# Down projection of a hybrid decoder layer: one group of nine block pairs in place of four, with its operands made ahead of time

## The chip, the cores and the metric

The kernel runs on one core of a Trainium2 chip. The metric is the device time of one launch in microseconds (us). Three runs of the kernel before took 1814.7, 1817.64 and 1820.21 us, so its median is 1817.64 us.

## The reference

One decoder layer over 1024 tokens and 16 learned tokens ahead of them, all in float32. The part that the change touches is the last line but one: the feed-forward network, whose inner width is 2816 (22 blocks of 128).

```python
h = h + concat([stick_breaking_attention, ssd_mixer, mla_attention]) @ w_out
fn = rmsnorm(h, ffn_norm_g)
h = h + (silu(fn @ w_gate) * (fn @ w_up)) @ w_down     # w_down: 2816 x 1024
return rmsnorm(h, final_norm_g)
```

## The kernel before

**Stages.** The kernel runs through these stages in order, with some overlap: projections and the stick-breaking attention, called the attention stage here (scores from 85 to 463 us), whose gaps on TensorE are filled with the projections of the convolution (`conv_unit`, 12 units); the state-space part (501 to 659 us); the second attention (MLA, 690 to 1024 us); the output projection; gate and up projection, called the gate stage (matmuls of `GateUp` from 1108.6 to 1555 us); the down projection, called the down stage (1555 to 1755 us); and the last part, which does four remaining blocks of the down projection and the final norm (to 1817 us). Tokens lie along the free dimension, features on the 128 partitions.

**Products.** A float32 operand is split into `hi` (ScalarE, called ACT, casts it to the type that TensorE multiplies) and `lo` (the rest, a subtraction on VectorE, called DVE, or on GpSimd, called POOL). A product is three matmuls: hi·hi, lo·hi and hi·lo.

**Gate and down stage.** Both use a scheme that multiplies 2 x 2 blocks with seven products instead of eight, at the price of sums of the blocks. The products carry the numbers 1 to 7. For the down projection a block pair `p` is two blocks of 128 of the inner width: the weights `w_down[2p]`, `w_down[2p+1]` (each 128 x 1024, two halves) and the hidden rows of the same two blocks. Product 1 takes plain blocks; 2 and 3 take plain inputs, 2 and 4 plain weights; the others take sums of blocks. One product of a pair is 12 matmuls of 128 x 512 into four PSUM banks (`product`).

**The gate stage's units.** `GateUp(p)`, p = 0 to 10, makes the hidden rows of pair p. `out(q)` ends each quarter: a sigmoid on ACT, two multiplications on DVE, and a store of the quarter `gs` to `s_hid` in DRAM from the queue of SyncE, called SP. The quarters end in the order 0, 3, 1, 2.

**The down stage.** `down_group(p0, n)` runs four times, with 2, 2, 2 and 3 pairs. It loads raw weights and hidden rows of its pairs (512 KB each), makes the sums for one product after another on DVE (`sub` and `add`, L1081 and L1084, in place in `raw` and in the tiles `tt`), splits both operands (casts on ACT L1077; `lo` of the weights on POOL L1078, of the inputs on POOL or DVE, by `LO_DVE`), and after each product adds the four banks into the residual `hF` on DVE (`gather`, L1084, with the loop `for o in range(4)`). Product 1 goes to `E1`, which POOL adds to `hF` at the end of all groups. Matmuls: L1496 to L1498.

**Order.** Every engine and the SP queue do their instructions in the order of the program. That order is set by a scheduler that places instructions by a priority (mostly the order in the code) and by its own estimate of when each is ready. A tile's tag with `bufs` buffers is handed out in turn: a new user waits until the last one is done. The value loads of the attention (`load_value_steps`) stage their raw data in two tiles, tags `vst` and `vsp`, one buffer each.

Of the kernel before, what the change touches and what calls it, by code (L numbers as in the profile page):

```python
# [21 lines left out]
KT = D // 128  # L22
# [36 lines left out]
def tile_hybrid_block(ctx: ExitStack, tc: tile.TileContext, a: dict):  # L59
# [588 lines left out]
    with ctx_sb as st:  # L648
# [27 lines left out]
        def sb_attend(p, proj, values):  # L676
            Q, K, KS = proj
            for h in range(2):
                for j in range(NQ // 2):
                    rows = [sb_row(Q[h], K[h], KS[h], 2 * j + e) for e in range(2)]  # L680
                    weighted_values(tp, pvp, sbb, j, rows, values[0], h, [x[p, 64 * h : 64 * (h + 1)] for x in (s_osbh, s_osbl)], pms[j % 2], values[1])

        values = load_value_steps(sbv, sbb, 0)
        step_sizes()
        convs = [8, 9, 10, 11, 0, 1, 2, 3, 4, 5, 6, 7]
        for p in range(4):
            sb_attend(p, proj, values)
# [548 lines left out]
    class GateUp:  # L1236


        def __init__(self, p):
            self.p = p  # L1240
            self.before = {}
            self.w, self.raw = [], []

        def load_early(self):
# [191 lines left out]
    f2 = ctx.enter_context(tc.tile_pool(name="f2", bufs=1, reuse_waits="tile"))  # L1436
    nraw = nop = 0

    def next_raw(src):
        nonlocal nraw  # L1440
        pl = fr if nraw % 16 < 8 else f2
        nraw += 1
        return raw_tile(pl, src)

    def operand():
        nonlocal nop
        t = fo.tile([128, 1024], F32R, tag="op", bufs=4, name="op") if nop % 16 >= 12 else hid_tile("op")
        nop += 1
        return t[:, HALF[0]], t[:, HALF[1]]
# [5 lines left out]
    LO_DVE = (1, 6, 2)  # L1455

    def down_group(p0, n):
        W, H = [], []
        for e in range(n):
            w, h = ([next_raw(src[2 * (p0 + e) + i]) for i in range(2)] for src in (a["w_down"], s_hid))  # L1460
            W.append((w[0][:, HALF[0]], w[1][:, HALF[0]], w[0][:, HALF[1]], w[1][:, HALF[1]], q_tile("tt")))
            H.append((h[0][:, HALF[0]], h[0][:, HALF[1]], h[1][:, HALF[0]], h[1][:, HALF[1]], q_tile("tt")))

        def operands(i):
            out = []
            for (a11, a12, a21, a22, tw), (b11, b12, b21, b22, th) in zip(W, H):
                if i == 6:
                    sub(a21, a11, a21)
                    sub(b12, b22, b12)
                    sub(tw, a22, a21)  # L1470
                    add(th, b12, b11)
                elif i == 5:
                    add(a11, tw, a11)
                    sub(b11, b22, th)
                elif i == 3:
                    sub(a12, a12, tw)
                elif i == 4:
                    sub(th, b21, th)
                left = {1: a11, 6: tw, 2: a12, 5: a11, 7: a21, 3: a12, 4: a22}[i]
                right = {1: b11, 6: th, 2: b21, 5: b11, 7: b12, 3: b22, 4: th}[i]  # L1480
                if p0 == 0 and i == 1:
                    hl = [wa.tile([128, 1024], F32R, tag=f"w{x}", name=f"w{x}") for x in ("hi", "lo")]
                    pair = [[t[:, s] for t in hl] for s in HALF]
                else:
                    pair = [operand(), operand()]
                split(*pair[0], left, pool)
                split(*pair[1], right, dve if i in LO_DVE else pool)
                out.append(pair)
            return out

        def product(i, banks, start):
            for e, ((wh, wl), (hh, hl)) in enumerate(operands(i)):
                for o in range(4):
                    os = slice(128 * o, 128 * (o + 1))
                    first, last = start and e == 0, e == n - 1
                    pe.matmul(banks[o], wh[:, os], hh, start=first, stop=False, skip_group_check=not start)  # L1496
                    pe.matmul(banks[o], wl[:, os], hh, start=False, stop=False, skip_group_check=not start)  # L1497
                    pe.matmul(banks[o], wh[:, os], hl, start=False, stop=last, skip_group_check=not start)  # L1498

        lo, hi = HALF  # L1500
        A = banks4()
        product(1, A, True)
        if p0 == 0:
            for k in range(KT):
                sp.dma_start(hT[k], s_h[k])
        for o in range(4):
            if p0 == 0:
                act.copy(E1[o], A[o])
            else:
                add(E1[o], E1[o], A[o])  # L1510
        B = banks4()
        product(6, B, True)
        gather(B, 4, lo)
        product(2, A, False)
        gather(A, 0, lo)
        product(5, B, False)
        gather(B, 4, hi)
        C = banks4()
        product(7, C, True)
        gather(C, 4, hi)  # L1520
        product(3, B, False)
        gather(B, 0, hi)
        product(4, C, False)
        gather(C, 4, lo)

    p0 = 0
# [10 lines left out]
    for e, f in enumerate(range(2 * p0, NF)):  # L1537
        w, h = next_raw(a["w_down"][f]), next_raw(s_hid[f])
        if e < 2:
            hl = [wa.tile([128, 1024], F32R, tag=f"w{x}", name=f"w{x}") for x in ("hi", "lo")]  # L1540
            split(*hl, w, pool)
            W = [[t[:, s] for t in hl] for s in HALF]
        else:
            W = [operand() for _ in HALF]
            for x, s in zip(W, HALF):
                split(*x, w[:, s], pool)
        H = [operand() for _ in HALF]
        for x, s in zip(H, HALF):
            split(*x, h[:, s], dve)
        last.append((W, H))  # L1550

    def down(o, t0, n):
        ts = slice(t0, t0 + n)
# [166 lines left out]
```

## Time and profile before

| what | number |
|---|---|
| runs | 1814.7, 1817.64, 1820.21 us |
| profiled execution | 1819.26 us, of which the trace's span is 1817.3 us |
| busy over the span | PE 95%, PEld 83%, DVE 67%, ACT 47%, POOL 47% |
| mean granted TensorE clock | 0.972 |
| bytes moved | 186.93 MB, mean 103 GB/s |
| chain that ended last | PE 68%, DVE 17%, ACT 4%, issue 3%, DMA 3%, POOL 3% |

PE is TensorE's matmuls, PEld its weight loads, which run beside the matmuls. A busy PE isn't a PE at its peak, since matmuls overlap: where nothing waits, the matmuls of 128 x 512 follow each other at less time than each one's own length. So the number of matmuls in a stretch, not its busy share, tells how far PE was held up there.

### The profile page before, as it was taken

What the parts mean: (1) busy time and instruction counts of PE and PEld (TensorE: products, weight loads), DVE (VectorE), ACT (ScalarE), POOL (GpSimd) and SP (SyncE); (2) the same over time, 40 slices, a digit from 0 to 9 for tenths busy, and PEclk for the clock granted to TensorE, in tenths of its full rate; (3) what the DMA queues carried; (4) which work ended last, traced back from release to release, by engine and by line L of the source; (5) the groups of instructions that cost most, each with busy time, mean ns of one, the idle gap of its engine ahead of it and who ended that gap; (6) DMA issues with size and microseconds to landing.
All of it is one profiled execution on the core that took longest, in us unless ns stands there. A gap on an engine that the chain in (4) does not pass through costs nothing.

```text
span 1817.3 us, 26447 instructions
## 1 busy us (share of the span) xinstructions
PE 1722.8 (95%) x9769; PEld 1506.0 (83%) x9769; DVE 1214.3 (67%) x1801; ACT 860.0 (47%) x1878; POOL 858.4 (47%) x597
## 2 busy tenths in 40 slices
PE   7969999999999999999999998999999999799997
PEld 7859998999987778998888876778888888677787
DVE  8686655777544673455576558967776667899854
ACT  7545564555566646775544424422232223334333
POOL 4433334343366557563321345634333234678783
PEclk9969999999998999999999998999999999899999
DMA  4211232222443546347221342232222233733102
GB/s 157 60 53 44 78 88 73 64 70 66 116 148 106 187 159 171 103 124 263 78 88 53 108 140 102 64 99 83 80 76 81 71 98 140 286 100 95 47 1 93
DMA packets 121012, 186.93 MB, mean 103 GB/s; under 512 B 21986, under 2 KB 81412, under 8 KB 120884
## 3 DMA queue, kind: packets, MB, share of 16 engines
q1 hardware_dynamic: 101488, 169.69, 29.6%
q10 hardware_dynamic: 19396, 15.56, 2.8%
q8 instruction: 77, 1.26, 0.3%
q14 instruction: 51, 0.42, 0.1%
HBM read 131.61 MB, written 53.60 MB: 102 GB/s over the span
## 4 chain that ended last, share of the span: by engine, by line
PE 68%; DVE 17%; ACT 4%; issue 3%; DMA 3%; POOL 3%; SPq 1%; ACTq 0%; DVEq 0%; POOLq 0%
PE d_ps L142 8%; PE d_ps L143 8%; PE d_ps L144 8%; PE b_ps L1295 7%; PE b_ps L1297 7%; PE b_ps L1296 7%; DVE raw L1081 2%; PE ptg L317 2%; PE b_ps L1498 1%; PE b_ps L1497 1%; PE ptg L319 1%; PE pv L295 1%; PE b_ps L1496 1%; PE pv L296 1%; DVE hF L1084 1%
## 5 line engine op out<-in xcount | busy, mean ns | idle before, releaser
L142 PE MATMUL d_ps<-hnh,whi 128*128 128x384 f32 (+6 forms) x744 | 247.3, 333 | 1.4 <-DVE go L534 0.7
L144 PE MATMUL d_ps<-hnl,whi 128*128 128x384 f32 (+6 forms) x744 | 246.7, 332 | 0.0
L143 PE MATMUL d_ps<-hnh,wlo 128*128 128x384 f32 (+6 forms) x744 | 245.6, 330 | 0.0
L131 POOL TENSOR_TENSOR wlo<-wraw,whi 128x1024 fp32r<-128x1024 f32 (+1 forms) x57 | 135.9, 2385 | 212.0 <-ACT whi L129 203.1
L1078 POOL TENSOR_TENSOR op<-raw,op 128x512 fp32r<-128x512 f32 x83 | 125.2, 1534 | 42.1 <-ACT op L1077 38.9
L142 PEld LDWEIGHTS d_ps<-hnh,whi 128*128 128x128 f32 (+1 forms) x744 | 140.4, 189 | 5.5 <-DVE go L534 1.3
L144 PEld LDWEIGHTS d_ps<-hnl,whi 128*128 128x128 f32 (+1 forms) x744 | 140.6, 189 | 3.3 <-issue 1.0
L143 PEld LDWEIGHTS d_ps<-hnh,wlo 128*128 128x128 f32 (+1 forms) x744 | 140.4, 189 | 2.3 <-issue 0.2
L1295 PE MATMUL b_ps<-T,wh 128*128 128x512 f32 x352 | 138.4, 393 | 0.9 <-DVE u L1084 0.9
L1296 PE MATMUL b_ps<-T,wl 128*128 128x512 f32 x352 | 138.1, 392 | 0.0
L1297 PE MATMUL b_ps<-T,wh 128*128 128x512 f32 x352 | 138.0, 392 | 0.0
L303 DVE TENSOR_TENSOR pl<-ptg,ph 128x512 fp32r<-128x512 f32 (+1 forms) x160 | 99.6, 628 | 46.3 <-ACT ph L302 44.7
L1078 POOL TENSOR_TENSOR wlo<-raw,whi 128x1024 fp32r<-128x1024 f32 (+1 forms) x22 | 52.7, 2395 | 152.9 <-ACT whi L1077 152.9
L669 DVE TENSOR_TENSOR_SCAN cm<-cm,zcol 128x144 f32<-128x144 f32 (+3 forms) x64 | 103.9, 1634 | 17.8 <-ACT cm L667 17.4
L1077 ACT CAST op<-raw 128x512 fp32r<-128x512 f32 x107 | 61.4, 618 | 96.7 <-PE d_ps L1498 49.4
L302 ACT CAST ph<-ptg 128x512 fp32r<-128x512 f32 (+1 forms) x160 | 85.3, 541 | 36.3 <-PE ptg L319 24.7
L1078 POOL TENSOR_TENSOR wl<-raw,wh 128x512 fp32r<-128x512 f32 x46 | 69.8, 1526 | 58.8 <-ACT wh L1077 58.0
L1084 DVE TENSOR_TENSOR hF<-hF,b_ps 128x512 f32<-128x512 f32 (+1 forms) x96 | 59.2, 635 | 46.4 <-PE b_ps L1562 23.9
L486 DVE SCALAR_TENSOR_TENSOR cacc<-d_ps,cw,cacc 128x384 f32<-128x384 f32 (+3 forms) x108 | 61.8, 572 | 38.2 <-ACT cacc L479 36.2
L1077 ACT CAST wh<-raw 128x512 fp32r<-128x512 f32 x88 | 52.9, 616 | 67.0 <-PE b_ps L1297 64.0
L129 ACT CAST whi<-wraw 128x1024 fp32r<-128x1024 f32 (+1 forms) x57 | 58.9, 1033 | 49.4 <-PE d_ps L144 23.4
L1496 PE MATMUL b_ps<-op 128*128 128x512 f32 x183 | 72.8, 401 | 9.9 <-DVE hF L1084 6.2
(452 smaller groups left out, 5352.8 us busy)
## 6 DMA issues: line engine op xcount, KB each, us to landing
raw<-in_w_gate_dram SPq DMA_DIRECT2D x22, 512.0 KB
raw<-in_w_up_dram SPq DMA_DIRECT2D x22, 512.0 KB, 4.1
s_hid<-gs SPq DMA_DIRECT2D x44, 256.0 KB, 2.4
raw<-in_w_down_dram SPq DMA_DIRECT2D x22, 512.0 KB, 5.2
raw<-s_hid SPq DMA_DIRECT2D x22, 512.0 KB, 4.3
wraw<-in_w_o_dram SPq DMA_DIRECT2D x16, 512.0 KB, 4.0
wraw<-in_w_xbc_dram SPq DMA_DIRECT2D x12, 512.0 KB, 3.8
s_xs<-csig SPq DMA_DIRECT2D x24, 192.0 KB, 2.6
```

What stands on the lines that cost most here:

```text
L131: pool.tensor_tensor(lo[:, :cols], raw[:, :cols], f32(hi[:, :cols]), op=ALU.subtract)
L142: pe.matmul(ps[:m, :n], wh, mh, start=(kt == 0), stop=False)
L143: pe.matmul(ps[:m, :n], wl, mh, start=False, stop=False)
L144: pe.matmul(ps[:m, :n], wh, ml, start=False, stop=(kt == nkt - 1))
L303: dve.tensor_tensor(pl[:, :n], pt[:, :n], f32(ph[:, :n]), op=ALU.subtract)
L669: dve.tensor_tensor_scan(rev, rev, zcol.to_broadcast([128, n_all]), 1.0, ALU.mult, ALU.add)
L1077: act.copy(hi, value)
L1078: eng.tensor_tensor(lo, value, f32(hi), op=ALU.subtract)
L1295: pe.matmul(banks[j], hi[:, ks], UH[u][k], start=start and k == 0, stop=False, skip_group_check=skip)
L1296: pe.matmul(banks[j], lo[:, ks], UH[u][k], start=False, stop=False, skip_group_check=skip)
L1297: pe.matmul(banks[j], hi[:, ks], UL[u][k], start=False, stop=stop and k == 3, skip_group_check=skip)
L1496: pe.matmul(banks[o], wh[:, os], hh, start=first, stop=False, skip_group_check=not start)
```

## The change

**In the attention stage** a new function `down_sums(p, c)` is called three times after each `conv_unit`, for 36 units in all (9 pairs, 4 column blocks). Each loads two pieces of `w_down` (128 KB each), makes the four sums of weights with four POOL operations of 128 x 128, and stores them (256 KB) in `s_wsum`. Its tile shares the tags `vst` and `vsp`.

**In the gate stage** `out` of the first nine units keeps its quarters `gs` and calls `hid_sums(q)`: four POOL operations of 128 x 512 make the sums of the inputs in place, and seven stores of 256 KB go to `s_hops` where four went to `s_hid`.

**In the down stage** there is one group of nine pairs. `operands(i, p)` loads one tile of 128 x 1024 for each product of each pair: the weights of that product on the left (from `w_down`, or from `s_wsum` in runs of 512 bytes) and its inputs on the right (from `s_hops`), two DMAs of 256 KB. One ACT cast makes `hi` for both, POOL makes `lo` of the weights, DVE `lo` of the inputs. No sums are left here, and `gather` runs 7 times, not 28. The order of the products is 1, 6, 2, 5, 7, 3, 4 as before, but each runs over all nine pairs. POOL's additions of `E1` to `hF` move from the end to behind product 1.

```diff
-    s_hid = dram.tile([NF, 128, SEQ], F32, name="s_hid")
+    s_hops = dram.tile([NS, 8, 128, 512], F32, name="s_hops")
+    s_wsum = dram.tile([NS, 4, 128, 4, 128], F32, name="s_wsum")
+    s_hid = dram.tile([NF - 2 * NS, 128, SEQ], F32, name="s_hid")
...
+        def down_sums(p, c):
+            w = sbb.tile([128, 5, 2, 64], F32, tag=("vst", "vsp")[c % 2], bufs=1, name="wd")
+            w = w.rearrange("p b h d -> p (b h d)")[:, :512].rearrange("p (q n) -> p q n", q=4)
+            for e in range(2):
+                src = a["w_down"][2 * p + e].rearrange("p (h c n) -> p h c n", h=2, c=4)
+                sp.dma_start(w[:, e::2], src[:, :, c])
+            for out, x, y, op in ((2, 0, 2, ALU.subtract), (3, 3, 2, ALU.subtract), (0, 0, 3, ALU.add), (1, 1, 3, ALU.subtract)):
+                pool.tensor_tensor(w[:, out], w[:, x], w[:, y], op=op)
+            sp.dma_start(s_wsum[p, c], w)
...
             for u in convs[3 * p : 3 * p + 3]:
                 conv_unit(u)
+                for x in sums[:3]:
+                    down_sums(*x)
+                del sums[:3]
...
-            sp.dma_start(s_hid[2 * self.p + q // 2, :, HALF[q % 2]], h)
+            if self.p >= NS:
+                sp.dma_start(s_hid[2 * (self.p - NS) + q // 2, :, HALF[q % 2]], h)
+            else:
+                self.h[q] = h
+                self.hid_sums(q)
+
+        def hid_sums(self, q):
+            h = self.h
+            if q in (0, 2, 3):
+                self.store({0: 1, 2: 2, 3: 3}[q], h[q])
+            if q == 1:
+                into(h[1], h[3], h[1], ALU.subtract)
+                self.store(7, h[1])
+                into(h[0], h[1], h[0], ALU.add)
+                self.store(6, h[0])
+                into(h[3], h[3], h[0], ALU.subtract)
+                self.store(5, h[3])
+            if q == 2:
+                into(h[2], h[2], h[0], ALU.subtract)
+                self.store(4, h[2])
...
-    for n in (2, 2, 2, 3):
-        down_group(p0, n)
-        p0 += n
+    def operands(i, p):
+        raw = next_raw()
+        if i in (1, 2, 4):
+            sp.dma_start(raw[:, HALF[0]], a["w_down"][2 * p + (i != 1)][:, HALF[i == 4]])
+        else:
+            src = s_wsum[p, :, :, {5: 0, 3: 1, 7: 2, 6: 3}[i]]
+            sp.dma_start(raw[:, HALF[0]].rearrange("p (c n) -> p c n", c=4), src.rearrange("c p n -> p c n"))
+        sp.dma_start(raw[:, HALF[1]], s_hops[p, i])
+        if i == 1 and p < 2:
+            hi, lo = (wa.tile([128, 1024], F32R, tag=f"w{x}", name=f"w{x}") for x in ("hi", "lo"))
+        else:
+            hi, lo = operand(), operand()
+        act.copy(hi, raw)
+        for s, eng in zip(HALF, (pool, dve)):
+            eng.tensor_tensor(lo[:, s], raw[:, s], f32(hi[:, s]), op=ALU.subtract)
+        return hi, lo
...
+    product(1, A, True)
...
+    for o in range(4):
+        act.copy(E1[o], A[o])
+    B = banks4()
+    product(6, B, True)
+    gather(B, 4, lo)
     for o in range(4):
         for ot, c in ((o, 1), (o + 4, 0), (o + 4, 1)):
             add(hT[ot][:, HALF[c]], hT[ot][:, HALF[c]], E1[o], pool)
+    product(2, A, False)
...
```

There are 16 raw tiles and 16 operand tiles in the down stage before and after (two more of each kind of operand tile from the weights' own pool for the first two pairs), so with two operand tiles for a pair's product the operands can be at most eight pairs ahead of PE.

The order on POOL in the attention stage, behind the first loads of the values (`vst`, `V`); `oTs` is the attention's output, `wlo` a split of weights for the projections. Before:

```order
L405 TENSOR_TENSOR vst<-vsp,vst 128x512
L354 TENSOR_TENSOR V<-vst,V 128x8x64
L346 TENSOR_TENSOR oTs<-oT,oTs 64x256 x2
L131 TENSOR_TENSOR wlo<-wraw,whi 128x1024
L346 TENSOR_TENSOR oTs<-oT,oTs 64x256
L131 TENSOR_TENSOR wlo<-wraw,whi 128x1024
```

and after, where `wd` are the new sums:

```order
L410 TENSOR_TENSOR vst<-vsp,vst 128x512
L696 TENSOR_TENSOR wd<-wd 128x128 x4
L359 TENSOR_TENSOR V<-vst,V 128x8x64
L351 TENSOR_TENSOR oTs<-oT,oTs 64x256
L696 TENSOR_TENSOR wd<-wd 128x128
L351 TENSOR_TENSOR oTs<-oT,oTs 64x256
L696 TENSOR_TENSOR wd<-wd 128x128 x9
L136 TENSOR_TENSOR wlo<-wraw,whi 128x1024
L696 TENSOR_TENSOR wd<-wd 128x128 x4
L351 TENSOR_TENSOR oTs<-oT,oTs 64x256
L696 TENSOR_TENSOR wd<-wd 128x128 x11
L136 TENSOR_TENSOR wlo<-wraw,whi 128x1024
```

The sums stand ahead of the splits of weights: 14 of them ahead of the first split shown and 15 between it and the second; later in the stage up to 19 stand between two splits.

The order on DVE where the down stage begins; `u` and `gs` are the last unit's outputs, `hF<-hF,b_ps` the first `gather`. Before:

```order
L1081 TENSOR_TENSOR tt<-raw 128x512
L1084 TENSOR_TENSOR tt<-raw 128x512
L1081 TENSOR_TENSOR tt<-raw 128x512
L1084 TENSOR_TENSOR tt<-raw 128x512
L1084 TENSOR_TENSOR u<-u,b_ps 128x512
L1084 TENSOR_TENSOR raw<-tt,raw 128x512
L1081 TENSOR_TENSOR raw<-raw,tt 128x512
L1084 TENSOR_TENSOR raw<-tt,raw 128x512
L1081 TENSOR_TENSOR raw<-raw,tt 128x512 x2
```

and after:

```order
L1323 TENSOR_TENSOR gs<-u,sig 128x512
L1104 TENSOR_TENSOR u<-u,b_ps 128x512
L1324 TENSOR_TENSOR gs<-gs,u 128x512
L1519 TENSOR_TENSOR op<-raw,op 128x512 x16
L1104 TENSOR_TENSOR hF_16141<-hF_16141,b_ps 128x512
L1519 TENSOR_TENSOR op<-raw,op 128x512
L1104 TENSOR_TENSOR hF_16142<-hF_16142,b_ps 128x512
```

The block sums ahead of the second product are gone; what is left are `lo` splits, which wait for nothing but their cast, and the gathers.

The order on POOL at the same place, after the change, where the additions of `E1` (in `grow` and `E`) to `hF` now stand; before, they stood behind the last split of the last group:

```order
L1519 TENSOR_TENSOR op<-raw,op 128x512 x8
L1104 TENSOR_TENSOR hF_16137<-hF_16137,grow 128x512
L1104 TENSOR_TENSOR hF_16141<-hF_16141,grow 128x512
L1104 TENSOR_TENSOR hF_16138<-hF_16138,grow 128x512
L1104 TENSOR_TENSOR hF_16142<-hF_16142,grow 128x512
L1519 TENSOR_TENSOR op<-raw,op 128x512
L1104 TENSOR_TENSOR hF_16139<-hF_16139,E_16145 128x512
L1104 TENSOR_TENSOR hF_16143<-hF_16143,E_16145 128x512
L1104 TENSOR_TENSOR hF_16140<-hF_16140,E_16145 128x512
L1104 TENSOR_TENSOR hF_16144<-hF_16144,E_16145 128x512
L1519 TENSOR_TENSOR op<-raw,op 128x512 x12
```

Twelve splits stand ahead of the first of these additions (the eight shown, and four above them), so the thirteenth pair's `lo` of the weights now stands behind four of them and the fourteenth's behind eight.

More of the change, by code (lines that the diff above doesn't have):

```diff
@@ L35 @@
 NF = D_FF // 128
+NS = 9
 EPS = 1e-6
@@ L681, in sb_attend @@
                     weighted_values(tp, pvp, sbb, j, rows, values[0], h, [x[p, 64 * h : 64 * (h + 1)] for x in (s_osbh, s_osbl)], pms[j % 2], values[1])
+        def down_sums(p, c):
[7 more added lines that the diff above has]
+            sp.dma_start(s_wsum[p, c], w)
+        sums = [(p, c) for p in range(NS) for c in range(4)]
         values = load_value_steps(sbv, sbb, 0)
@@ L1240, in __init__ @@
             self.p = p
-            self.before = {}
+            self.before, self.h = {}, {}
             self.w, self.raw = [], []
@@ L1304, in out, with store, into @@
             dve.tensor_tensor(h, h, up, op=ALU.mult)
-            sp.dma_start(s_hid[2 * self.p + q // 2, :, HALF[q % 2]], h)
+            if self.p >= NS:
[3 more added lines that the diff above has]
+                self.hid_sums(q)
+        def store(self, i, h):
+            sp.dma_start(s_hops[self.p, i], h)
+        def hid_sums(self, q):
+            h = self.h
+            def into(out, x, y, op):
+                pool.tensor_tensor(out, x, y, op=op)
+            if q in (0, 2, 3):
[10 more added lines that the diff above has]
+                self.store(4, h[2])
         def top(self):
@@ L1437, in tile_hybrid_block, with next_raw @@
     nraw = nop = 0
-    def next_raw(src):
+    def next_raw():
         nonlocal nraw
@@ L1442, in next_raw @@
         nraw += 1
-        return raw_tile(pl, src)
+        return raw_tile(pl)
     def operand():
@@ L1454, in tile_hybrid_block @@
     E1 = [t[:, s] for t in (grow, both) for s in HALF]
[L1455 to L1524, printed above, removed]
@@ new lines, in product @@
+    def product(i, banks, start):
+        for p in range(NS):
+            hi, lo = operands(i, p)
+            hh, hl = hi[:, HALF[1]], lo[:, HALF[1]]
+            for o in range(4):
+                os = slice(128 * o, 128 * (o + 1))
+                first, last = start and p == 0, p == NS - 1
+                pe.matmul(banks[o], hi[:, os], hh, start=first, stop=False, skip_group_check=not start)
+                pe.matmul(banks[o], lo[:, os], hh, start=False, stop=False, skip_group_check=not start)
+                pe.matmul(banks[o], hi[:, os], hl, start=False, stop=last, skip_group_check=not start)
@@ L1531, in tile_hybrid_block @@
+    lo, hi = HALF
+    A = banks4()
+    product(1, A, True)
+    for k in range(KT):
+        sp.dma_start(hT[k], s_h[k])
+    for o in range(4):
+        act.copy(E1[o], A[o])
+    B = banks4()
+    product(6, B, True)
+    gather(B, 4, lo)
     for o in range(4):
@@ L1533, in tile_hybrid_block @@
             add(hT[ot][:, HALF[c]], hT[ot][:, HALF[c]], E1[o], pool)
-    last = []
[L1537 to L1550, printed above, removed]
+    product(2, A, False)
+    gather(A, 0, lo)
+    product(5, B, False)
+    gather(B, 4, hi)
+    C = banks4()
+    product(7, C, True)
+    gather(C, 4, hi)
+    product(3, B, False)
+    gather(B, 0, hi)
+    product(4, C, False)
+    gather(C, 4, lo)
+    last = []
+    for f in range(2 * NS, NF):
+        parts = []
+        for src, eng in ((a["w_down"][f], pool), (s_hid[f - 2 * NS], dve)):
+            raw = next_raw()
+            sp.dma_start(raw, src)
+            hi, lo = operand(), operand()
+            act.copy(hi, raw)
+            for s in HALF:
+                eng.tensor_tensor(lo[:, s], raw[:, s], f32(hi[:, s]), op=ALU.subtract)
+            parts.append([(hi[:, s], lo[:, s]) for s in HALF])
+        last.append(parts)
     def down(o, t0, n):
```

3 lines of the change are left out of this document (1 added, 2 removed).

## Prediction, made blind

> **What bounds the kernel now.** I read the page first: PE is busy for 95% of the span, so only a stage in which PE waits can give time back. Next I cut the span by stage. The columns are the window and its length, the busy time and number of instructions of each engine, the granted TensorE clock, the DMA share and GB/s.
>
> ```profile
> 160.00:510.00 350.00, 345.58 (x2382) 334.56 (x2381) 234.07 (x330) 194.13 (x436) 145.50 (x108) 1.00 0.29 84
> ...
> 1200.00:1550.00 350.00, 350.00 (x1514) 283.69 (x1513) 237.78 (x278) 102.93 (x167) 124.72 (x73) 1.00 0.27 88
> 1555.00:1600.00 45.00, 34.88 (x143) 27.56 (x142) 41.99 (x43) 18.28 (x33) 37.30 (x24) 0.89 0.77 284
> 1600.00:1650.00 50.00, 43.36 (x184) 33.40 (x183) 50.00 (x64) 17.35 (x31) 36.15 (x24) 1.00 0.28 85
> 1650.00:1700.00 50.00, 46.85 (x192) 37.31 (x191) 46.38 (x59) 19.97 (x34) 41.36 (x26) 0.93 0.27 84
> 1700.00:1755.00 55.00, 55.00 (x244) 45.55 (x243) 37.55 (x46) 21.70 (x38) 49.86 (x37) 1.00 0.12 39
> 1755.00:1817.00 62.00, 52.75 (x350) 48.15 (x349) 23.25 (x48) 19.11 (x39) 27.23 (x29) 0.94 0.19 68
> ```
>
> The four rows from 1555 to 1755 are the down stage. In the last of them PE never rests and does 244 matmuls of 128x512 in 55.00 us: 0.2254 us a step. The four rows hold 143 + 184 + 192 + 244 = 763 matmuls, and 763 x 0.2254 = 172.0 us. The stage takes 200, so 28.0 us are lost there. In the first three rows DVE is busy for 41.99 of 45, 50.00 of 50 and 46.38 of 50 us. The waits from 1555 to 1700 name it (columns: total us, times, longest):
>
> ```profile
> PE b_ps L1498 <- DVE op L1078: 6.5, 1, 6.5
> PE b_ps L1496 <- DVE hF L1084: 6.2, 5, 1.8
> ...
> PE d_ps L1496 <- DVE hF L1084: 3.5, 4, 1.7
> ...
> PE b_ps L1496 <- ACT grow L1508: 2.7, 2, 1.5
> ```
>
> These are 18.9 of the lost us, all but 2.7 on DVE; the wait for `grow` is on the copy of product 1. The rest is slow clock: 0.89 over 45 us and 0.93 over 50 us are 4.95 + 3.5 = 8.5 us. How a wait turns into slow clock stands in the timeline (start, length):
>
> ```profile
> 1687.24 0.39 PE L1498 MATMUL b_ps<-op 128*128 128x512 f32 x1
> 1689.43 0.65 PE L1496 MATMUL b_ps<-op 128*128 128x512 f32 x1 [1.81 <-DVE hF L1084]
> 1689.88 0.63 PE L1497 MATMUL b_ps<-op 128*128 128x512 f32 x1
> ...
> 1696.51 0.40 PE L1498 MATMUL b_ps<-op 128*128 128x512 f32 x1
> ```
>
> After a wait of 1.81 us the step is 0.43 to 0.45 us, until 1696.5, for some 7 us: it costs up to 3.4 us more.
>
> **The down stage after the change.** PE's count stays: 9 pairs x 7 products x 12 = 756 matmuls. One pair's product takes PE 12 x 0.2254 = 2.70 us. What the others need for it:
>
> ```profile
> L1084 DVE TENSOR_TENSOR hF<-hF,b_ps 128x512 f32<-128x512 f32 x72 | 47.1, 678 | 20.4 <-PE b_ps L1498 20.3
> L1078 DVE TENSOR_TENSOR op<-raw,op 128x512 fp32r<-128x512 f32 x22 | 25.2, 1161 | 2.3 <-ACT op L1077 2.3
> L1081 DVE TENSOR_TENSOR raw<-raw,tt 128x512 f32<-128x512 f32 x18 | 23.0, 1284 | 0.0
> ...
> L1078 POOL TENSOR_TENSOR op<-raw,op 128x512 fp32r<-128x512 f32 x83 | 125.2, 1534 | 42.1 <-ACT op L1077 38.9
> ...
> L129 ACT CAST whi<-wraw 128x1024 fp32r<-128x1024 f32 (+1 forms) x57 | 58.9, 1033 | 49.4 <-PE d_ps L144 23.4
> ```
>
> - Removed from DVE: the sums (L1081 and L1084 on `raw` and `tt`, the third row being one kind of them, 23 us) and 84 of 112 gathers, 84 x 0.678 = 57 us.
> - DVE after: one `lo` of 1.16 us per pair, 63 in all, 73 us, and 28 gathers, 19 us: 92 of 172 us. It no longer bounds.
> - POOL: 1.53 of 2.70 us. ACT: one cast of 128x1024, 1.03 us by the nearest row of that shape.
> - Loads: 63 x 512 KB = 33.0 MB in 172 us is 192 GB/s. By the first row of the down stage (0.77 for 284) this is a share of 0.52, by the second (0.28 for 85) 0.63: under 1 both ways. Pieces of 512 bytes for 36 of the 63 weight halves speak for the upper end.
>
> So every engine keeps pace with PE, with operands up to eight pairs (21.6 us) ahead. Four losses are left.
>
> - Transition from the gate stage: the 6.5 us wait was for a DVE `lo` behind sums. Now 16 `lo` wait for casts alone, behind the gate's last outputs. Bounds 0 and 6.5; I take 1.
> - POOL's additions of `E1`, moved behind product 1:
>
> ```profile
> L1084 POOL TENSOR_TENSOR hF<-hF,grow x6: 1292/1312/1752, 1737.9 to 1758.5; 128x512 f32<-128x512 f32 x6
> L1084 POOL TENSOR_TENSOR hF<-hF,E x6: 1296/1298/1744, 1742.0 to 1761.0; 128x512 f32<-128x512 f32 x6
> ```
>
>   Minimum, median and maximum ns are 1.3 to 1.75 us. Product 1 ends at 9 x 2.70 = 24.3 us after its start, its first bank some 2 us earlier; with the copy the first addition can start at 23. Four additions (5.2) and a split (1.5) end at 29.7: the 13th pair's `lo`, needed at 12 x 2.70 = 32.4, is in time. The next four and a split end at 36.4 (38.9 at 1.5 us and more each, with a slow split); the 14th pair needs it from 13 x 2.70 + 0.2 = 35.3. PE waits 1 to 4 us; I take 2. No other work is held: the first `gather` waits for product 6. Off the end of the stage go the 12 additions, which lay beside PE.
> - Slow clock behind that wait: 0 to 3.4 us by the timeline; I take 1.5, since the row's wait is of the same size but the clock stayed at 1.00 in the window 1600:1650, which has waits too.
> - The end: the four remaining blocks want all operand tiles of product 4's last pairs, and DVE stands behind 4 gathers (2.7 us): 0 to 3, taken as 1.5.
>
> For the third of these the Trainium skill has a rule. TensorE: Matmul & The Clock Gate, section "Part 1: The HAM clock gate", says that the clock drops to half only after an idle window of about 3.4 us. This trace does not agree, as the wait of 1.81 us shows; by the page's rule, as an estimate, the forecast would be 1.5 us lower.
>
> Together 6 of the 28.0 us stay, and the stage gives back 22 (28 at most; by the upper ends of the four, 17 or so are lost and 11 come back).
>
> **The attention stage.** Added are 36 x 4 = 144 POOL operations, 72 loads and 36 stores on SP. No row has a sum of 128x128; these are nearest:
>
> ```profile
> L405 POOL TENSOR_TENSOR vst<-vsp,vst 128x512 f32<-128x512 f32 x8 | 10.2, 1279 | 25.2 <-DMA vsp<-s_vsb 13.7 <-DMA vst<-s_vsb 11.4
> ...
> L405 POOL TENSOR_TENSOR vst<-vsp,vst 16x128 f32<-16x128 f32 x8 | 3.6, 448 | 11.0 <-DMA vsp<-s_vsb 6.7 <-DMA vst<-s_vsb 4.0
> ```
>
> The second has the same 128 elements in each partition, so I take 0.45; the other end is 1.28. Then POOL gets 65 us (184 at most) beside 145.50 of 350: at most 330, still under. The queue:
>
> ```profile
> s_hid<-gs SPq DMA_DIRECT2D x44, 256.0 KB, 2.4
> ...
> vst<-s_vsb SPq DMA_DIRECT2D x8, 256.0 KB, 3.8
> ```
>
> A unit is load 3.8, four sums 1.8, store 2.4: 8.0 us on one buffer; with two buffers taken in turn 4.0 us per unit, 144 us in all. SP waits for each, and the weight loads of the projections stand behind; a weight is needed about every 15 us:
>
> ```profile
> 142.73 2.40 POOL L131 TENSOR_TENSOR wlo<-wraw,whi 128x1024 fp32r<-128x1024 f32 x1 [8.90 <-ACT whi L129]
> ...
> 157.30 2.38 POOL L131 TENSOR_TENSOR wlo<-wraw,whi 128x1024 fp32r<-128x1024 f32 x1 [9.53 <-ACT whi L129]
> ```
>
> POOL sits idle 9 us for each, 14.6 us apart. Nineteen sums between two splits, the most that the order shows, are 4.75 units or 19 us at 4.0 each: 4.4 us over that pace, and a split is ready about one weight ahead. PE itself hardly waits here: 345.58 of 350 us, with these as its largest waits:
>
> ```profile
> PE ptm L307 <- DVE cm L669: 2.0, 1, 2.0
> PE ptg L317 <- DVE pm L310: 1.2, 1, 1.2
> ```
>
> Cost: 0 if the lead covers it, 5 places x 4.4 = 22 if it never does; it is nearer to covered, since matmuls of the scores stand between those of the projections and can be taken in their place. DVE slows a little beside POOL. I take 2.
>
> **The gate stage.** Added are 9 x 4 POOL operations and 27 stores of 256 KB.
>
> ```profile
> 1342.16 2.41 POOL L1078 TENSOR_TENSOR wlo<-raw,whi 128x1024 fp32r<-128x1024 f32 x1 [13.47 <-ACT whi L1077]
> ```
>
> Four at 1.3 to 1.5 are 6 us a unit, into an idle gap of 13.47 us. The quarters' buffers come free later, by the sums and a store of 2.4 us, while DVE's next use is a unit on, about 40 us (11 units from 1108.6 to 1555). PE is busy for 350.00 of 350 us. I take 0; ends 0 and 9 (1 us for each of nine units, the size by which a late `gs` could hold DVE).
>
> **Sum.** 1817.64 - 22 + 2 + 0 = 1797.6. The profiled execution took 1819.26 us, 1.6 above the median; the difference is put on the median. Forecast 1798, and 1789 to 1804 as this case's own range. A change under 0.3% (5.5 us) can't be told from none.
>
> **Rivals.**
> - Half the gain. Behind product 1 the eight loads of `hF` (512 KB each, 4.2 MB, 14.8 us at 284 GB/s) stand ahead of product 6's loads, and POOL adds there; if both use up the 21.6 us of lead, PE pays the upper ends of all four losses: 1817.64 - 11 + 2, about 1808. For it: the queue is in order. Against: 16 raw tiles allow loads far ahead.
> - No change, 1812 to 1823: the down stage gives 22 and the attention takes 22, the end worked out above. It decides once a split comes later than the 14.6 us lead.
> - Slower, by sums that hold up SP. If the two buffers don't overlap (the store of one ahead of the load of the next in SP's order), a unit takes 8.0 us, all 36 take 288, and 4.75 of them 38 us against about 30 that lead and pace give: 8 us of wait at five places, +40, with 22 back 1836. It decides from a unit of 6.3 us (30/4.75). For it: SP waits for POOL as it is; against: `vst` and `vsp` are two tags.
>
> ```profile
> SPq L127 <- POOL wlo L131: 82.5, 18, 11.0
> ```
>
> - Slower, by loads. If a raw tile's two 256 KB halves came one after the other, at 2.4 each by the `s_hid` row, a pair would take 4.8 us against 2.70: 63 x 4.8 = 302 in place of 172, about 1900. Against it: 284 GB/s in one window, several loads at once.
>
> The Trainium skill has a rule on this side too. DMA: Bandwidth & Descriptors, section "Bandwidth", asks for 1 MiB or more per DMA and gives 138 GB/s for 64 KB; at that rate, as an estimate, a pair's 512 KB takes 3.8 us and the stage 239, that is 1857. The row of 284 GB/s, made of 512 KB loads, speaks against it, though no row has loads of 512 bytes a piece at that pace.
>
> **Chances.** Forecast, 1789 to 1804: 0.60. Half, 1804 to 1812: 0.18. No change: 0.10. Held-up SP or POOL: 0.09. Loads: 0.03. That is faster 0.78, same 0.10, slower 0.12. The range for 8 in 10 runs from 1788 to 1814, forecast and half and a little of the third.
>
> **What would show it.** Right: the down stage's matmuls (L1529 to L1531 of the changed kernel) in some 178 us, clock 1.00 in nearly all of it, DVE idle there for casts, one PE wait for a POOL split at the 14th pair's product; in the attention stage PE waits still near 5 us; none in the gate stage. Wrong: PE waiting for matmuls with `wlo` in the attention stage, casts waiting for loads of `raw` in the down stage, or DVE waiting for POOL to let go of `gs` in the gate stage.

## The result, and the profile after

The changed kernel takes 1824.46 us (median of nine runs, 1821.79 to 1827.30), the kernel before 1819.16 in the runs beside them. The ratio is 1.0027 with an interval of 1.0014 to 1.0039: about 5 us slower, where 1798 was forecast. The profiled execution has a span of 1820.7 us against 1817.3.

First the places of the stages. These rows of the changed kernel hold the first and the last start of one group of matmuls each: scores of the first attention, scores of MLA, the gate's first group, the down stage, the last part.

```profile
L666 PE MATMUL sc_ps<-K,Q x112: 226/345/702, 85.6 to 480.1; 128*128 128x400 f32 x32, 128*128 128x272 f32 x24, 128*128 128x384 f32 x24, 128*128 128x256 f32 x16
L979 PE MATMUL sc_ps<-mhi x112: 229/358/483, 709.5 to 1043.7; 96*128 96x400 f32 x32, 96*128 96x272 f32 x24, 96*128 96x384 f32 x24, 96*128 96x256 f32 x16
L1315 PE MATMUL b_ps<-raw,whi x160: 390/394/476, 1129.5 to 1551.5; 128*128 128x512 f32 x160
L1529 PE MATMUL b_ps<-whi x6: 389/389/389, 1577.6 to 1581.7; 128*128 128x512 f32 x6
L1580 PE MATMUL b_ps<-op x96: 278/283/395, 1759.0 to 1807.9; 128*128 128x256 f32 x64, 128*128 128x512 f32 x32
```

The scores end at 480.1 instead of 463, MLA begins at 709.5 instead of 690, the gate stage at 1129.5 instead of 1108.6, the down stage at 1577.6 instead of 1555. The down stage then takes 181.4 us (1577.6 to 1759.0) instead of 200. So 19 us were won there and some 22 lost ahead of it, 19 of these by the start of MLA. The windows, as those of before:

```profile
160.00:510.00 350.00, 332.41 (x2275) 321.48 (x2274) 221.91 (x320) 186.99 (x427) 189.21 (x221) 0.99 0.39 116
1200.00:1550.00 350.00, 346.31 (x1494) 279.91 (x1493) 230.41 (x274) 101.64 (x164) 183.35 (x109) 1.00 0.31 103
1577.00:1600.00 23.00, 23.00 (x103) 19.06 (x102) 3.55 (x6) 3.55 (x4) 3.07 (x2) 1.00 1.00 352
1600.00:1640.00 40.00, 33.58 (x134) 26.84 (x134) 23.71 (x20) 17.73 (x21) 38.24 (x26) 0.91 0.77 245
1640.00:1758.00 118.00, 118.00 (x522) 97.68 (x521) 48.28 (x62) 45.72 (x44) 74.52 (x48) 1.00 0.46 139
```

In the attention stage PE does 2275 matmuls in 350 us where it did 2382. In the down stage DVE has dropped from 176 to some 76 us, PE runs through from 1640 on, and what is left of the loss lies between 1600 and 1640. There the DMA share has been 1.00 for 23 us just before, and the waits from 1577 to 1760 read:

```profile
ACT op L1517 <- DMA raw<-s_hops: 22.2, 6, 13.0
...
PE b_ps L1530 <- POOL op L1519: 6.4, 2, 5.7
```

POOL in that stretch, with the additions of `E1` (L1104) between the splits:

```profile
1598.71 5.22 POOL L1519 TENSOR_TENSOR op<-raw,op 128x512 fp32r<-128x512 f32 x3 [12.28 <-ACT op L1517]
1603.90 6.41 POOL L1104 TENSOR_TENSOR hF<-hF,grow 128x512 f32<-128x512 f32 x4
1610.27 1.73 POOL L1519 TENSOR_TENSOR op<-raw,op 128x512 fp32r<-128x512 f32 x1
1611.95 6.79 POOL L1104 TENSOR_TENSOR hF<-hF,E 128x512 f32<-128x512 f32 x4
1618.70 13.77 POOL L1519 TENSOR_TENSOR op<-raw,op 128x512 fp32r<-128x512 f32 x10
```

Two things meet there: the casts stand 13.0 us for late loads, and the splits that PE then waits for stand behind the additions.

### The profile page after: what moved, and what is told of

It is laid out like the page before. It is cut to its first block, busy times and chain, and to the rows that moved or that the text cites. A ratio compares the mean times of both kernels' runs of the same rounds, so it can differ in the third digit from the quotient of the medians.

```text
span 1820.7 us, 26880 instructions
## 1 busy us (share of the span) xinstructions
PE 1718.0 (94%) x9769; PEld 1504.6 (83%) x9769; DVE 1101.7 (61%) x1681; ACT 849.5 (47%) x1809; POOL 932.1 (51%) x743
## 4 chain that ended last, share of the span: by engine, by line
PE 63%; DVE 11%; POOL 7%; DMA 7%; ACT 6%; issue 5%; SPq 1%; ACTq 0%; POOLq 0%; DVEq 0%
PE d_ps L147 6%; PE b_ps L1315 6%; PE b_ps L1317 6%; PE b_ps L1316 6%; PE d_ps L148 6%; PE d_ps L149 6%; PE b_ps L1530 2%; PE b_ps L1531 2%; PE b_ps L1529 2%; POOL wd L696 2%; DMA wd<-in_w_down_dram 1%; PE ptg L322 1%; ACT L L796 1%; PE pv L301 1%; PE ptg L324 1%
## 5 line engine op out<-in xcount | busy, mean ns | idle before, releaser
L1519 POOL TENSOR_TENSOR op<-raw,op 128x512 fp32r<-128x512 f32 x61 | 97.9, 1615 | 58.4 <-ACT op L1517 57.4
L1519 DVE TENSOR_TENSOR op<-raw,op 128x512 fp32r<-128x512 f32 x61 | 64.4, 1066 | 84.4 <-ACT op L1517 84.4
L674 DVE TENSOR_TENSOR_SCAN cm<-cm,zcol 128x144 f32<-128x144 f32 (+3 forms) x64 | 100.6, 1577 | 22.7 <-ACT cm L672 22.5
L1517 ACT CAST op<-raw 128x1024 fp32r<-128x1024 f32 x61 | 63.6, 1053 | 106.7 <-PE d_ps L1531 75.0
L696 POOL TENSOR_TENSOR wd<-wd 128x128 f32<-128x128 f32 x144 | 81.6, 581 | 61.3 <-DMA wd<-in_w_down_dram 58.2
L1098 POOL TENSOR_TENSOR wlo<-raw,whi 128x1024 fp32r<-128x1024 f32 x18 | 45.5, 2528 | 96.6 <-ACT whi L1097 96.6
L1315 PEld LDWEIGHTS b_ps<-T,wh 128*128 128x128 f32 x352 | 66.1, 188 | 16.4 <-DVE u L1104 1.3
```

The costliest lines, as they stand in the source:

```text
L674: dve.tensor_tensor_scan(rev, rev, zcol.to_broadcast([128, n_all]), 1.0, ALU.mult, ALU.add)
L696: pool.tensor_tensor(w[:, out], w[:, x], w[:, y], op=op)
L1315: pe.matmul(banks[j], hi[:, ks], UH[u][k], start=start and k == 0, stop=False, skip_group_check=skip)
L1519: eng.tensor_tensor(lo[:, s], raw[:, s], f32(hi[:, s]), op=ALU.subtract)
```

## The experiments

Times are medians, ratios are against the kernel before run beside them; 0.001 is 1.8 us. Differences between variants are taken from the ratios; the intervals reach 2 to 6 us to each side.

| run | us | ratio | interval |
|---|---|---|---|
| changed kernel | 1824.46 | 1.0027 | 1.0014 to 1.0039 |
| no_sums | 1800.31 | 0.9908 | 0.9878 to 0.9937 |
| dma_only | 1811.31 | 0.9974 | 0.9959 to 0.9989 |
| pool_only | 1813.50 | 0.9975 | 0.9960 to 0.9991 |
| sums_alone | 1841.26 | 1.0142 | 1.0118 to 1.0166 |
| sums_mla | 1837.95 | 1.0124 | 1.0092 to 1.0156 |
| store_pool | 1819.46 | 1.0014 | 1.0003 to 1.0025 |
| e1_dve | 1820.01 | 1.0019 | 1.0008 to 1.0029 |
| mla_e1 | 1835.95 | 1.0103 | 1.0080 to 1.0126 |
| hf_late | 1814.46 | 0.9981 | 0.9970 to 0.9992 |
| half | 1815.08 | 0.9987 | 0.9972 to 1.0002 |
| stpool_hf | 1813.40 | 0.9970 | 0.9955 to 0.9984 |
| spread_pool_hf | 1819.64 | 1.0008 | 0.9994 to 1.0022 |
| no_sums_hf | 1791.41 | 0.9858 | 0.9825 to 0.9891 |
| pin_sp | 1793.81 | 0.9878 | 0.9844 to 0.9911 |
| pin_pool | 1804.90 | 0.9933 | 0.9910 to 0.9955 |
| pin_load | 1794.78 | 0.9867 | 0.9841 to 0.9892 |

### Where the loss is

no_sums takes the calls of `down_sums` out:

```diff
-                for x in sums[:3]:
-                    down_sums(*x)
-                del sums[:3]
...
-            src = s_wsum[p, :, :, {5: 0, 3: 1, 7: 2, 6: 3}[i]]
+            src = a["w_down"][2 * p + i % 2].rearrange("p (c n) -> p c n", c=8)[:, i // 4 :: 2]
```

The four products whose weights were sums multiply plain blocks here.

> The changed kernel without down_sums in the attention stage; the down stage's weight halves of products 5, 3, 7 and 6 come from w_down in the same pieces of 512 bytes, so its values are others. All theories that put the cost of the change into the attention stage: the scores end near 463 us as before, not 480, the down stage keeps its 181 us, and the time is about 1805 us (17 to 20 below the changed kernel). If the loss behind 1050 us is a cost of the gate's sums: about 1808. If the attention isn't the cause: 1824.

0.9908: the sums in the attention stage cost 0.0119, 22 us. The rest of the change, gate stage included, is worth 17 us. Nearly all of the 22 us are lost between 300 and 420 us. First no_sums, then the changed kernel:

```profile
300.00:420.00 120.00, 119.92 (x800) 116.34 (x799) 89.87 (x124) 68.18 (x150) 50.31 (x34) 1.00 0.21 66
```

```profile
300.00:420.00 120.00, 104.27 (x664) 98.86 (x663) 68.94 (x103) 56.47 (x128) 85.25 (x114) 0.97 0.48 150
```

PE does 136 of 800 matmuls fewer, a sixth of 120 us.

sums_alone puts `down_sums` and its calls into the kernel before.

> The kernel before with down_sums in the attention stage and nothing else of the change; what it stores is not read. If the attention's cost is of the sums alone: 17 us above the kernel before, a ratio of 1.009, scores to 480 us. If it comes of the order that the scheduler finds with the rest of the change: under 5 us.

1.0142, 26 us above the kernel before: the cost needs nothing else of the change.

dma_only and pool_only leave one half of each unit:

```diff
-            for out, x, y, op in (...):
-                pool.tensor_tensor(w[:, out], w[:, x], w[:, y], op=op)     # dma_only
...
-                sp.dma_start(w[:, e::2], src[:, :, c])                     # pool_only
-            sp.dma_start(s_wsum[p, c], w)                                  # pool_only
-                pool.tensor_tensor(w[:, out], w[:, x], w[:, y], op=op)     # pool_only
+                pool.tensor_tensor(w[:, out], ident, ident, op=op)         # pool_only
```

> down_sums with its loads and stores, without its four POOL operations (what is stored are the plain blocks). Theory 1, POOL stands waiting for the loads of the sums and holds up its other work: nothing waits on POOL any more, about 1807 us. Theory 2, SP is held up by the sums' loads and stores and the weights come late: the cost stays, about 1822. Theory 3, POOL's added work slows DVE and itself: about 1807.

> down_sums with its four POOL operations, reading a constant tile, without loads and stores; the down stage reads its weights as in no_sums. Theory 1: POOL has 65 us more to do but never waits for a load: about 1808 us. Theory 2: about 1805. Theory 3: the cost stays, about 1822.

Against no_sums each half costs 12 us (0.0066 and 0.0067), together the whole. None of the three theories had expected two equal halves. In dma_only SP shows a price. `wlo` of one weight is done at 363.1, which frees the raw buffer, and SP, between loads and stores of the sums, issues the next weight's load 12 us later:

```profile
360.71 2.39 POOL L136 TENSOR_TENSOR wlo<-wraw,whi 128x1024 fp32r<-128x1024 f32 x1 [0.55 <-ACT whi L134]
```

```profile
367.15 1.57 SPq L695 DMA_DIRECT2D s_wsum<-wd  x2
369.35 2.12 SPq L694 DMA_DIRECT2D wd<-in_w_down_dram  x3
372.16 0.60 SPq L694 DMA_DIRECT2D wd<-in_w_down_dram  x1
373.17 1.87 SPq L695 DMA_DIRECT2D s_wsum<-wd  x2
375.09 0.42 SPq L132 DMA_DIRECT2D wraw<-in_w_xbc_dram  x1
```

In pool_only nearly all splits follow their casts at once, and PE's longest wait between 300 and 480 us is 4.6 us for a scan on DVE. That scan is long beside the sums. First pool_only, in which POOL works without a pause from 308.90 to 314.86, then the same scan in no_sums:

```profile
309.26 7.25 DVE L674 TENSOR_TENSOR_SCAN cm<-cm,zcol 128x784 f32<-128x784 f32 x1
```

```profile
308.69 1.78 DVE L674 TENSOR_TENSOR_SCAN cm<-cm,zcol 128x784 f32<-128x784 f32 x1
```

All 64 scans take 109 us instead of 104. The scores end 9 us later than in no_sums, MLA starts 14 us later: the rest is lost in the state-space stage, where one split of a weight starts 8.5 us behind its cast, and 1.5 in no_sums; ahead of it on POOL stands other work that itself waits 7.1 us. Whether DVE's 5 us account for the 9 is not shown.

### What it is: two trials that missed

sums_mla moves the units into MLA, one behind each block; store_pool issues the stores from POOL:

```diff
+            if c % 2:
+                w = ml.tile([128, 5, 2, 64], F32, tag="vst", bufs=1, name="wd")...
+            else:
+                w = ml.tile([128, 512], F32, tag="wd", bufs=1, name="wd")
...
-            sp.dma_start(s_wsum[p, c], w)       # store_pool
+            pool.dma_start(s_wsum[p, c], w)     # store_pool
```

> The changed kernel with the 36 units of down_sums moved from the attention stage to the second attention (MLA), about one behind each of its 32 blocks, in a tile of its own and in the tag vst of that stage. Theory Q, the sums cost time because they stand in the queues of POOL and SP that feed the weights of the projections (one raw buffer, one weight every 15 us), which the second attention does not load: nearly all of the attention's 24 us come back, about 1803 us. Theory W, the work itself (POOL beside DVE, 28 MB more traffic) slows the kernel wherever it stands: about 1818 to 1825.

> The changed kernel with the 36 stores of the sums issued from POOL's queue, behind its own operations, so that SP never waits for a sum. Theory Q-SP, the larger part is weight loads behind SP's waits for POOL: about 1812 us. Theory Q-POOL, POOL's own queue is the larger part and gets the issue of the stores on top: 1825 us or more.

sums_mla is slower still, 1.0124, 39 us above no_sums. The stretch of MLA, too, has work on POOL that PE waits for behind another engine (`gy` on POOL, then `go` on DVE, of the projections that fill its gaps), and POOL stands as long for the sums' loads as in the attention stage. The scores of MLA end 5 us later than in no_sums, the gate stage begins 31 us later. First POOL's waits from 690 us on, then PE's:

```profile
POOL wd L1013 <- DMA wd<-in_w_down_dram: 54.2, 26, 7.2
```

```profile
PE d_ps L147 <- DVE go L539: 9.3, 9, 2.6
```

store_pool won some 2 us, within the intervals, and fits neither of its theories; SP's waits for the sums alone don't make the loss.

half keeps 18 of the 36 units (its expectation says 16; the trace has 18 stores of sums); spread_pool_hf puts one unit behind each attention block, with the three edits of stpool_hf (below):

```diff
-                for x in sums[:3]:
+                for x in sums[:3][: 1 + u % 2]:                          # half
...
+                    for x in sums[: 2 if j == 0 and h else 1]:           # spread_pool_hf, in sb_attend
+                        down_sums(*x)
```

> The changed kernel with 16 of the 36 units of down_sums (one or two behind each convolution unit; the down stage's halves of products 5, 3, 7 and 6 are read from w_down). If each unit costs the same (24 us / 36 = 0.67 us): 1800 + 11 = 1811 us. If the cost begins only where more units stand between two weights than the lead covers, 16 units cost little: under 1804.

> The same three edits, and one unit of down_sums behind each of the 32 blocks of the first attention, in place of three behind each convolution unit. If bursts of sums are what costs, 4 to 8 us less than stpool_hf, about 1805 us; if only their number counts, the same 1811.

half costs 14 us against no_sums, where half of 22 is 11, a difference within the intervals; spreading made it 7 us worse than stpool_hf. Read alone, both speak for a price per unit wherever it stands. The trace of half allows another reading: ten of its 18 units stand between 294 and 379 us, and up to 14 sums still stand between two splits (19 in the changed kernel). Its cast and its split of one weight (first ACT, then POOL):

```profile
362.31 1.05 ACT L134 CAST whi<-wraw 128x1024 fp32r<-128x1024 f32 x1
```

```profile
378.49 2.33 POOL L136 TENSOR_TENSOR wlo<-wraw,whi 128x1024 fp32r<-128x1024 f32 x1
```

15 us lie between the end of the cast and the split. The changed kernel has the same. Its ACT, with the casts of two weights and what ACT waits for next:

```profile
352.84 1.05 ACT L134 CAST whi<-wraw 128x1024 fp32r<-128x1024 f32 x1
373.30 0.58 ACT L605 CAST Q<-d_ps 64x512 fp32r<-64x512 f32 x1 [8.27 <-DMA wraw<-in_w_xbc_dram]
373.78 1.04 ACT L134 CAST whi<-wraw 128x1024 fp32r<-128x1024 f32 x1
394.27 0.67 ACT L484 ACTIVATE cacc<-d_ps,cb,cw 128x384 f32<-128x384 f32 x1 [9.08 <-DMA wraw<-in_w_xbc_dram]
```

and its POOL in the same stretch:

```profile
355.57 0.47 POOL L696 TENSOR_TENSOR wd<-wd 128x128 f32<-128x128 f32 x1 [4.88 <-DMA wd<-in_w_down_dram]
...
362.84 3.60 POOL L696 TENSOR_TENSOR wd<-wd 128x128 f32<-128x128 f32 x5 [2.79 <-DMA wd<-in_w_down_dram]
366.40 2.33 POOL L136 TENSOR_TENSOR wlo<-wraw,whi 128x1024 fp32r<-128x1024 f32 x1
368.70 2.77 POOL L696 TENSOR_TENSOR wd<-wd 128x128 f32<-128x128 f32 x6
376.11 5.39 POOL L696 TENSOR_TENSOR wd<-wd 128x128 f32<-128x128 f32 x6 [4.63 <-DMA wd<-in_w_down_dram]
...
387.72 2.39 POOL L136 TENSOR_TENSOR wlo<-wraw,whi 128x1024 fp32r<-128x1024 f32 x1
```

The cast of 352.84 gets its split at 366.40, that of 373.78 at 387.72: 13 us late each, behind sums and the loads that these wait for. The weights have a single raw buffer, so the next load goes out only then (at 368.76 and 390.14), and ACT, in order, stands 8 to 9 us for its landing with the attention's own work behind it. So PE is held up through ACT and DVE, and hardly by the split itself: from 120 to 540 us it waits 23 us in all (9.5 in the kernel before), and for `wlo` only once:

```profile
PE d_ps L148 <- POOL wlo L136: 2.1, 1, 2.1
```

The weights follow each other in 21 us. Without sums (no_sums, POOL) they do so in 18 and 16:

```profile
350.82 2.40 POOL L136 TENSOR_TENSOR wlo<-wraw,whi 128x1024 fp32r<-128x1024 f32 x1 [8.06 <-ACT whi L134]
368.97 2.38 POOL L136 TENSOR_TENSOR wlo<-wraw,whi 128x1024 fp32r<-128x1024 f32 x1
385.40 2.39 POOL L136 TENSOR_TENSOR wlo<-wraw,whi 128x1024 fp32r<-128x1024 f32 x1 [1.31 <-ACT whi L134]
```

### The down stage

e1_dve moves POOL's additions of `E1` to DVE; hf_late leaves them and issues the loads of `hF` behind those of product 6. mla_e1 is sums_mla with e1_dve's edit; stpool_hf has the edits of store_pool, hf_late and e1_dve.

```diff
-            add(hT[ot][:, HALF[c]], hT[ot][:, HALF[c]], E1[o], pool)     # e1_dve
+            add(hT[ot][:, HALF[c]], hT[ot][:, HALF[c]], E1[o], dve)
...
-    for k in range(KT):                                                  # hf_late
-        sp.dma_start(hT[k], s_h[k])
     for o in range(4):
         act.copy(E1[o], A[o])
     B = banks4()
     product(6, B, True)
+    for k in range(KT):
+        sp.dma_start(hT[k], s_h[k])
```

> The changed kernel with the 12 additions of E1 on DVE instead of POOL. If PE's wait of 5.7 us in the down stage and the slow clock behind it (0.93 over 45 us, 3 us) come from these additions ahead of the split of the 14th pair, 6 to 9 us come back: about 1817 us, no PE wait for POOL there. If they come from late loads: 1824 us.

> The changed kernel with the eight loads of hF behind the loads of product 6 on SP, not ahead of them. Theory H: PE's wait of 5.7 us in the down stage comes from operands of product 6 that land late behind the 4.2 MB of hF; then the casts' wait of 13.0 us for raw goes, PE waits under 2 us there and 6 to 9 us come back, about 1817 us. Theory E: it is the additions of E1 on POOL; then the wait stays or grows, since they now wait for hF: 1824 or more.

In e1_dve the wait changed its name, not its size; the gain of 1.5 us isn't clear of the intervals:

```profile
PE b_ps L1531 <- DVE op L1519: 6.4, 2, 6.0
```

By itself this doesn't clear the additions: they now stand on DVE ahead of the split that PE waits for, and the casts stand 13.0 us for loads as before.

hf_late gained 0.0046, 8.4 us, with the additions still on POOL. The casts' wait for `raw` from 1577 on is 9.6 us in all instead of 22.2, the longest 5.7 instead of 13.0, and from 1585 to 1765 PE never rests and keeps its clock:

```profile
ACT op L1517 <- DMA raw<-s_hops: 9.6, 5, 5.7
```

```profile
1585.00:1765.00 180.00, 180.00 (x795) 148.94 (x794) 73.84 (x91) 71.23 (x72) 121.60 (x78) 1.00 0.57 184
```

795 matmuls in 180 us are 0.2264 us each, the full rate (the last 13 us are of the last part). The down stage takes 171.5 us (1580.4 to 1751.9) instead of 181.4. So the additions cost PE something only where the operands come late.

> Both edits, sums in the second attention and additions of E1 on DVE. If they are independent and both theories hold: 1803 - 8, about 1795 us, 23 below the kernel before. If the second attention pays for the sums: 1812 or more.

> Stores of the sums from POOL's queue, hF's loads behind product 6's, E1 on DVE. If the three gains add up: 1819.5 - 4 - 5, about 1811 us, below the kernel before (1818).

mla_e1 is 1.0103, with the loss of sums_mla. stpool_hf is 0.9970, 8 us under store_pool, as hf_late is under the changed kernel.

### Sums tied to the weights

no_sums_hf is no_sums with hf_late's edit. pin_sp is hf_late with each unit's POOL operations and store ordered behind a certain weight's split, two units for each weight, and the loads of the next two placed there too. The weights of keys and queries get units as well, so the sums also spread over more weights. pin_pool stores from POOL; pin_load issues the loads inside the same tie as the operations.

```diff
+        weights.append(last_on(mybir.EngineType.Pool))     # in load_w, behind the split
...
+        def down_sums(more=True):
+            with tc.issue_after(weights[-1]):
+                for p, c, w in pend:
+                    for out, x, y, op in (...):
+                        pool.tensor_tensor(w[:, out], w[:, x], w[:, y], op=op)
+                    sp.dma_start(s_wsum[p, c], w)
+            pend.clear()
+            if more:
+                down_load()                                 # loads of the next two units
```

> no_sums (no down_sums, the halves of products 5, 3, 7 and 6 read from w_down) with hF's loads behind product 6's: the floor for any placing of the sums. If the gain of hf_late (8 to 10 us) adds to that of no_sums: about 1792 us.

> hf_late with the sums tied to the weights in the first attention: behind each weight's split on POOL stand the operations of two units at most, whose loads were issued a weight earlier. Theory P, the cost is the splits of weights that stand behind up to 22 sums and their loads on POOL (cast at 373.78, split at 387.72 in the changed kernel): a split starts at most 6 us behind its cast, the weights keep the pace of 16 us that they have without sums, and most of the 22 us come back: 1795 to 1802 us. Theory W, each unit costs its 0.67 us wherever it stands: 1814, as hf_late.

> The same with the stores of the sums issued from POOL's queue. If SP's waits for POOL still matter when the sums are tied: 3 us below pin_sp; if not, the issues cost POOL 36 x 0.56 us and it is 0 to 3 us above.

> pin_sp with the loads of a unit issued with its own operations, not a weight earlier; the order on POOL is that of pin_sp. Theory P1, what counts is how many sums stand ahead of a split: as pin_sp, about 1795 us. Theory P2, what counts is that POOL doesn't stand waiting for the loads of the sums (13.5 us in pin_sp, 58 in the changed kernel): that wait grows again and the time with it, 1802 or more.

pin_sp is at 0.9878, 19 us under hf_late and 0.0020 above no_sums_hf, the floor, though all 36 units are done in the same stage. Theory P holds, with a time 1 us below its range. From 300 to 420 us PE does 770 matmuls, where no_sums does 800 and the changed kernel 664:

```profile
300.00:420.00 120.00, 116.54 (x770) 112.28 (x769) 87.12 (x122) 67.28 (x148) 85.19 (x103) 1.00 0.46 146
```

In the stretch shown above its splits follow their casts by 1 us or less (4.9 at most in the whole stage), 19 and 16 us apart (ACT, then POOL):

```profile
371.05 1.05 ACT L136 CAST whi<-wraw 128x1024 fp32r<-128x1024 f32 x1
388.14 1.04 ACT L136 CAST whi<-wraw 128x1024 fp32r<-128x1024 f32 x1
```

```profile
354.13 2.41 POOL L138 TENSOR_TENSOR wlo<-wraw,whi 128x1024 fp32r<-128x1024 f32 x1 [0.64 <-ACT whi L136]
...
373.05 2.38 POOL L138 TENSOR_TENSOR wlo<-wraw,whi 128x1024 fp32r<-128x1024 f32 x1
...
389.25 2.39 POOL L138 TENSOR_TENSOR wlo<-wraw,whi 128x1024 fp32r<-128x1024 f32 x1 [1.41 <-ACT whi L136]
```

pin_pool is 10 us slower than pin_sp, more than the 0 to 3 expected. Three of its splits between 317 and 381 us start 3.2 to 5.9 us behind their casts, where those of pin_sp follow at once. pin_load equals pin_sp, but it didn't make the loads later: POOL waits 12.5 us for them where it waits 13.5 in pin_sp. So it leaves open how much of the 19 us is the limit of two units, how much the loads' place and how much the spread over more weights. The changed kernel had 58.2 us of these waits, pin_sp has 13.5:

```profile
POOL wd L696 <- DMA wd<-in_w_down_dram: 58.2, 29, 5.2
```

```profile
POOL wd L707 <- DMA wd<-in_w_down_dram: 13.5, 13, 3.2
```

pin_sp is the version to keep: 1793.81 us, 1.2% under the kernel before.

## Why the prediction was wrong

**The down stage, 22 us back: close.** The ceiling of 28.0 us was right (with `hF` out of the way the stage takes 171.5 us, 172.0 in the prediction), and so were the relief of DVE and the unchanged count. 19 came back: 9.4 us stayed lost where the sum had 6. PE waited just where the prediction put it, for the two splits behind the additions of `E1`, but for 6.4 us instead of 2, and the clock of 0.91 over 40 us behind it is 3.6 us instead of 1.5. Transition and end cost nothing, against 2.5 in the sum. What failed in this term is the lead: the sum had product 6's operands made up to eight pairs ahead of PE, but their casts stood 13.0 us for loads, which came behind those of `hF`. That is the mechanism of the rival "half the gain". It took the loads of `hF` for 14.8 us at 284 GB/s, under the 21.6 us of lead; at the stage's start product 1's loads were still on the way beside them, at a share of 1.00 for 23 us.

The slow clock there fits the Trainium skill, TensorE: Matmul & The Clock Gate, section "Part 1: The HAM clock gate", which asks for an idle window of about 3.4 us: the wait of 5.7 us was longer. The wait of 1.81 us in the kernel before, with steps of 0.43 us behind it, still does not fit.

**Transfers.** Serial loads didn't come true: 352 GB/s at a share of 1.00, with pieces of 512 bytes among them. (That rival's own figures, 302 us in place of the stage's 200, give some 1920 us, not 1900.)

**The attention stage, 2 us: this step failed; 22 us were measured.** The parts were nearly right: the additions of 128 x 128 have a median of 0.46 us (0.45 taken; with some long ones the mean is 0.58, 82 us in all where 65 were forecast), a unit takes 4 to 5 us where they stand densest (ten stores of sums from 353 to 400 us), up to 19 sums stand between two splits. The row of the profile with `wlo` at 14.6 us pace and 9 us of idle POOL was read, too. What was wrong is the step from there to the price: "a split is ready about one weight ahead", and PE can take scores in the meantime. The lead isn't kept: since there is one raw buffer, every split that comes late makes the next load late by as much, and the same ACT that waits for that load also serves the scores. So the sign that the prediction named, PE waiting for matmuls with `wlo`, stays small (2.1 us) while the stage loses some 20. hf_late and pin_sp, which do the same 36 units, differ by 19 us through the order of the sums, the place of their loads and their spread over the weights.

That the upper end of the bounds, 22 us, was the answer is luck: it was five places of 4.4 us, each where a split comes later than the 14.6 us of lead; in the trace no split comes more than 12.9 us behind its cast, and eight come 3 us or more behind. In the same way the rival "no change", down stage won and attention lost, given 0.10, has the outcome, with the sum a little over, but not the condition that it named.

The prediction also let DVE slow "a little" beside POOL, within the 2 us. pool_only shows one scan at 7.25 us instead of 1.78; what this is worth in the changed kernel is not shown, and pin_sp, with the same operations on POOL, comes within 0.0020 of the floor.

**The gate stage, 0 us: nearly.** Counted from the first matmul of each, the stage takes 448.1 us in the changed kernel and 446.6 in the kernel before, and 450.8 in no_sums: 1.5 to 4 us. Behind its first 100 us PE does the same 433 or 434 matmuls in each further 100 us in all three. (The windows from 1200 to 1550 above don't show that, since the later stage is cut at another place.) Yet the sign that the prediction named for this stage did come, DVE waiting for POOL to let go of `gs` (changed kernel, the whole stage):

```profile
DVE gs L1323 <- POOL gs L1340: 31.4, 7, 7.0
```

DVE had the room for it: PE's pace didn't change.

## What to carry to other kernels

Work put "into the idle time" of an in-order engine is paid for by what stands behind it, not by its own length: look for the instruction on that engine that frees a single buffer, and count how many new instructions, with the loads that they wait for, a scheduler can place ahead of it. Tie filler work to that instruction, a fixed small number behind each, with its loads issued earlier; here these three together took 19 us off at the same work, and which of them did most is open. And where a stage begins with a burst of loads, order the queue by the time at which each is needed, since the mean DMA share says nothing of the first 20 us.

## What the runs showed of the hardware that was not expected

Loads and stores without sums and sums without loads and stores cost 12 us each, and together the sum of both, though the first holds up SP and the second only POOL. A part of the second is seen: a scan of 128 x 784 on DVE took 7.25 us beside 6 us of unbroken work on POOL, 1.78 us without; the rest is open. Stores issued from POOL's queue, which made no difference clear of the intervals where POOL was badly ordered (2 us), cost 10 us where it was well ordered, with 0.56 us of POOL for each of the 36 issues. Sixteen loads of 256 KB and eight of 512 KB issued within 23 us from one queue, some in pieces of 512 bytes, moved 352 GB/s.
